# A hybrid encoder block on one core: the end of building h in halves and quarters with scans held, the passage from o to the gate by token tile, an even order in the inversions

## The chip, the cores and the metric

One core of one Trainium2 chip runs the whole kernel. The metric is the device time of one execution in microseconds (us). Three timed executions took 1959.03, 1960.29 and 1960.35 us; their median, 1960.29 us, is the time before. A fourth execution was profiled.

The engines have short names in the views: PE is TensorE (PEld its loads of stationary operands), DVE is VectorE, ACT is ScalarE, POOL is GpSimd, SP is SyncE, which issues most of the loads.

## The reference

```python
mod = silu(c) @ ada_w + ada_b                     # shift, scale, gate for mixer and FFN
h = rms_norm(x, norm_mix_w) * (1 + scale_m) + shift_m
proj = h @ w_in                                   # split into both branches, z, o, merge gates
h_a = bidirectional(mlstm_chunkwise, ...)         # 4 heads, dk 256, dv 512
y_a = (sigmoid(a_o) * rms_norm(h_a)) @ w_branch_a
o_b = bidirectional(gated_delta_chunkwise, ...)   # 16 heads, conv of 5, chunks, triangular solve
y_b = (rms_norm(o_b) * silu(b_z)) @ w_branch_b
x = x + gate_m * ((g_a * y_a + g_b * y_b) @ w_out)
hf = rms_norm(x, norm_ffn_w) * (1 + scale_f) + shift_f
gt, up = split(hf @ w_gate_up)
x = x + gate_f * ((silu(gt) * up) @ w_down)
return rms_norm(x, norm_final_w)
```

There are T = 256 tokens (two token tiles of 128) and D = 2048 features (KB = 16 blocks of 128). All is fp32.

## The kernel before

Every weight is read once from HBM, in pieces of 1 MB ("raw" tiles, three buffers, loads issued by SP). ACT rounds a half of a piece to fp32r (`wh`), DVE subtracts to get the rest (`wl = raw - wh`), and TensorE adds three products for one of fp32: wh with the high part of the activations, wh with their low part, wl with the high part. `wh` and `wl` have three buffers each. Two generators do this. `fjob` (L164) makes 128 output features with 256 tokens in a multiplication. `tjob` (L193) has a token tile as the stationary operand and 512 output features in a multiplication; it takes four pieces, so eight halves of 12 multiplications. With `by_token`, its last two halves are multiplied token tile by token tile, so that the first tile's result is done early.

Much of the rest of the work is latency: small operations that wait for one another. `fill(n)` puts n pieces of jobs between them, so that TensorE has something to do. Where `order(...)` is put around an instruction, it keeps its place in the program among those so marked on its engine; the others a scheduler places. `behind` and `settle()` hold back work, such as an evict or a SiLU, until the next half has its `wh`. `ask`, `add` and `pump` bring in the rows of ada_w for the later modulations, one 1 MB load and one DVE sum (`add`, L123) at a time.

The stages, by time in the profile:

* To 138 us, h. Per block b, SP loads two tiles of ada rows (`ra`, 1.025 MB each) and one 1 MB `raw` tile of w_in. DVE multiplies and sums the first (L519, its factor from `pk`, a table of constants) and the second (L523), and between them multiplies x by the row factors and the scale (L548). ACT adds the shift (L551) and rounds to `hh` (L552), DVE makes `hl` (L555), and TensorE adds 16 output tiles `first` in plain fp32 (L557, 32 multiplications). Table `cst` holds the identity, masks (`Dm`) and signs.
* To 300 us, `gates()` turns the first outputs into the decay and beta of the gated delta rule (GDN), with a z job and the q, k, v of the first heads between; `gdn_phase1` makes per head the decay matrices `dec` by four scans (L591 and on) and the masked products.
* To 940 us, four groups g of four heads. `invert(g)` solves the triangular 32x32 systems on DVE: 30 steps of a multiply-and-sum into `utmp` and an add into `uu` (L701, L707). The results go to DRAM (`inv_d`) and come back in another layout (`cg`, L720), and a transpose of `cg` (L722) starts `gdn_blocks`. POOL issues these transfers: the store once for the upper and once for the lower 16 rows, each as four (one per head of a group, 16 partitions each, in runs of 128 bytes); the load as four of 32 partitions in runs of 2 KB. A job is filled in between: in `gdn_invert`, a yield comes when a size that counts each step's elements plus 125 passes 580, and starts again at 0. In the groups' second half, `stream()` takes the next heads' jobs into the loops of `gdn_phase2` (n from 1 to 9, p 0 and 1).
* To 1200 us, the mLSTM branch and both branch projections.
* To 1260 us, `o_job` (the output projection), the residual and its RMS norm, and the transposes `pxn` of the normed x (L1341) into `hfh`, `hfl`, which the gate job `gt0` needs. `normed` (L1276 on DVE, L1278 on ACT) scales a token tile's columns; `block` and `pair` transpose two blocks of 128 features, both token tiles together, and scale them.
* To 1950 us, gate and up, then down; then the final norm.

## Time and profile before

| what | value |
|---|---|
| median of three executions | 1960.29 us |
| the profiled execution's own time | 1962.84 us |
| its span in the trace | 1961.0 us |
| TensorE busy | 1926.3 us, 98% |
| DVE busy | 1405.7 us, 72% |
| ACT busy | 1028.7 us, 52% |
| moved from and to HBM | 467.07 MB read, 16.82 MB written |
| mean granted clock of TensorE | 0.994 |

A row of a timeline has the start, the duration, engine, line of the code, operation, what it writes and reads, and, in brackets, how long the engine was idle before it and whose end released it. A row of a windows view has a stretch, its length, each engine's busy time with its number of instructions, the granted clock of TensorE (1.00 is full), the mean share of the DMA engines that were busy, and GB/s. A multiplication of 128x512 is shown with 0.38 us, because they overlap in a pipeline; the distance of two starts is what one costs.

### The profile page before, as it was taken

To read this page: it belongs to the slowest core of one execution; us is meant where nothing else is said; L and a number is where in the kernel's file an instruction comes from. 1 tells how busy PE (TensorE), PEld (TensorE's weight loads), DVE (VectorE), ACT (ScalarE), POOL (GpSimd) and SP (SyncE) were. 2 spreads that over 40 slices of the span, in tenths; PEclk is the share of its full clock that TensorE was granted. 3 is DMA by queue.
4 is the path that set the end of the run, shared out by engine and by line. 5 is a ranking of instruction groups with operands and counts; after the bars stand their busy time and mean duration, and the time that the engine had idled before them with its cause. 6 is when DMAs were issued, how large, how long until landed. Compare 5 with 4: busy or idle time off the path is not lost.

```text
span 1961.0 us, 27095 instructions
## 1 busy us (share of the span) xinstructions
PE 1926.3 (98%) x10418; PEld 1703.2 (87%) x10418; DVE 1405.7 (72%) x2067; ACT 1028.7 (52%) x1553; POOL 116.9 (6%) x211
## 2 busy tenths in 40 slices
PE   8999999999999999999999999999999999999997
PEld 6888889998999899889787888888888888888886
DVE  6779886898788788866677988665665665555554
ACT  3137656775776588555544444644444444444444
POOL 0001210101011101110100000200000000000000
PEclk9999999999999999999999999999999999999999
DMA  9986677666666667687777998566666665555553
GB/s 400 420 355 223 187 249 252 209 229 217 228 211 212 226 217 232 221 285 254 250 294 266 352 348 325 179 242 247 247 248 239 245 246 193 197 211 209 199 206 138
DMA packets 78962, 485.64 MB, mean 248 GB/s; under 512 B 10585, under 2 KB 15969, under 8 KB 24433
## 3 DMA queue, kind: packets, MB, share of 16 engines
q1 hardware_dynamic: 63216, 450.69, 63.0%
q0 software_dynamic: 8160, 17.88, 4.3%
q10 hardware_dynamic: 7458, 15.36, 2.0%
q8 instruction: 81, 1.33, 0.3%
q14 instruction: 47, 0.39, 0.1%
HBM read 467.07 MB, written 16.82 MB: 247 GB/s over the span
## 4 chain that ended last, share of the span: by engine, by line
PE 83%; DVE 7%; DMA 6%; ACT 2%; issue 2%; POOL 0%; SPq 0%; ACTq 0%; DVEq 0%; POOLq 0%
PE acc_gt L230 4%; PE acc_gt L231 4%; PE acc_gt L232 4%; PE acc_up L232 4%; PE acc_up L231 4%; PE acc_up L230 4%; PE acc_d L232 4%; PE acc_d L231 4%; PE acc_d L230 4%; DMA ra<-ada 3%; PE acc_b L183 3%; PE acc_b L185 3%; PE acc_b L184 3%; PE acc_o L232 3%; PE acc_o L230 3%; PE acc_o L231 2%
## 5 line engine op out<-in xcount | busy, mean ns | idle before, releaser
L211 DVE TENSOR_TENSOR wl_d<-raw_d,wh_d 128x1024 fp32r<-128x1024 f32 x88 | 107.7, 1225 | 105.9 <-ACT wh_d L209 105.9
L211 DVE TENSOR_TENSOR wl_up<-raw_up,wh_up 128x1024 fp32r<-128x1024 f32 x88 | 107.7, 1225 | 100.2 <-ACT wh_up L209 100.1
L211 DVE TENSOR_TENSOR wl_gt<-raw_gt,wh_gt 128x1024 fp32r<-128x1024 f32 x88 | 108.2, 1229 | 80.2 <-ACT wh_gt L209 80.2
L183 PE MATMUL acc_b<-hh,wh_b 128*128 128x256 f32 x576 | 163.2, 283 | 0.0
L185 PE MATMUL acc_b<-hh,wl_b 128*128 128x256 f32 x576 | 160.0, 278 | 0.0
L184 PE MATMUL acc_b<-hl,wh_b 128*128 128x256 f32 x576 | 159.5, 277 | 0.0
L209 ACT ACTIVATE wh_d<-raw_d 128x1024 fp32r<-128x1024 f32 x88 | 92.9, 1056 | 126.4 <-PE acc_d L231 117.6
L209 ACT ACTIVATE wh_gt<-raw_gt 128x1024 fp32r<-128x1024 f32 x88 | 92.9, 1055 | 118.6 <-PE acc_gt L231 71.1
L209 ACT ACTIVATE wh_up<-raw_up 128x1024 fp32r<-128x1024 f32 x88 | 92.8, 1055 | 108.1 <-PE acc_up L231 77.1
L123 DVE SCALAR_TENSOR_TENSOR ada<-ada,crow 128x2048 f32<-128x2048 f32 x64 | 146.1, 2283 | 0.0
L230 PE MATMUL acc_gt<-wh_gt,hfh 128*128 128x512 f32 x352 | 135.9, 386 | 0.0
L231 PE MATMUL acc_gt<-wh_gt,hfl 128*128 128x512 f32 x352 | 135.1, 384 | 0.0
L232 PE MATMUL acc_gt<-wl_gt,hfh 128*128 128x512 f32 x352 | 134.2, 381 | 0.0
L230 PE MATMUL acc_up<-wh_up,hfh 128*128 128x512 f32 x352 | 133.4, 379 | 0.0
L231 PE MATMUL acc_up<-wh_up,hfl 128*128 128x512 f32 x352 | 133.4, 379 | 0.0
L232 PE MATMUL acc_up<-wl_up,hfh 128*128 128x512 f32 x352 | 133.4, 379 | 0.0
L230 PE MATMUL acc_d<-wh_d,ffh 128*128 128x512 f32 x344 | 130.5, 379 | 0.0
L231 PE MATMUL acc_d<-wh_d,ffl 128*128 128x512 f32 x344 | 130.5, 379 | 0.0
L232 PE MATMUL acc_d<-wl_d,ffh 128*128 128x512 f32 x344 | 130.4, 379 | 0.0
L557 PE MATMUL first<-x,raw 128*128 128x256 f32 x512 | 114.5, 382 | 7.5 <-ACT x L551 7.5
L557 PEld LDWEIGHTS first<-x,raw 128*128 128x128 f32 x512 | 96.0, 190 | 26.0 <-ACT x L551 13.5
L183 PEld LDWEIGHTS acc_b<-hh,wh_b 128*128 128x128 f32 x576 | 111.9, 194 | 0.1
(383 smaller groups left out, 5258.0 us busy)
## 6 DMA issues: line engine op xcount, KB each, us to landing
ada<-ada SPq DMA_DIRECT2D x64, 1024.0 KB, 6.2
raw_gt<-wgu SPq DMA_DIRECT2D x44, 1024.0 KB, 5.0
raw_up<-wgu SPq DMA_DIRECT2D x44, 1024.0 KB, 4.9
raw_d<-wd SPq DMA_DIRECT2D x44, 1024.0 KB, 4.9
raw_b<-winb SPq DMA_DIRECT2D x36, 1024.0 KB, 5.3
ra<-ada SPq DMA_DIRECT2D x32, 1025.0 KB, 15.6
raw<-win SPq DMA_DIRECT2D x16, 1024.0 KB, 14.5
raw_z<-wint SPq DMA_DIRECT2D x16, 1024.0 KB, 5.1
```

The source lines that it names most:

```text
L123: order(V.scalar_tensor_tensor(raw, raw, 1.0, row_c[:, :D], ALU.mult, ALU.mult, accum_out=mod[:, c : c + 1]))
L183: PE.matmul(o, wh[:, k], woven(hh[:, kk]), start=kk == 0, stop=False)
L184: PE.matmul(o, wh[:, k], woven(hl[:, kk]), start=False, stop=False)
L185: PE.matmul(o, wl[:, k], woven(hh[:, kk]), start=False, stop=kk == KB - 1)
L209: order(S.activation(wh, raws[u][:, k0 : k0 + 2], AF.Copy), early)
L211: order(V.tensor_tensor(wl, raws[u][:, k0 : k0 + 2], wh.bitcast(F32), ALU.subtract), early)
L230: order(PE.matmul(ps[t], xh[:, kk, c], woven(wh[:, k]), start=kk == 0, stop=False), early and steps > 1)
L231: PE.matmul(ps[t], xl[:, kk, c], woven(wh[:, k]), start=False, stop=False)
L232: PE.matmul(ps[t], xh[:, kk, c], woven(wl[:, k]), start=False, stop=kk == last)
L557: PE.matmul(first[o], raw[:, o], x[:, b], start=b == 0 and o % 2 == 0, stop=b == KB - 1 and o % 2 == 1)
```

## The change

It has these parts.

* **Start.** ACT loads the identity, the 16 columns of `pk` that the h loop needs (`pkn`), and the last 13 columns of `cst`. All of `pk` is loaded by SP behind the last `raw` tile of h, the rest of `cst` behind z's first pieces.
* **h loop.** The multiply of x by the row factors is made a block ahead (`spread`), and the scale is applied by ACT together with the shift. An Exp on one column stands ahead of the loop.
* **Last block of h.** The `ra` tiles are loaded and summed in halves (1024 and 1026 columns, with an add of 128x1), and `raw` in quarters. Four of the 16 outputs stay fp32; the other twelve are split (`wh_first`, `wl_first`, three of 128x512 each) and take three fp32r multiplications each.
* **gates, phase 1.** In `gates`, the order of Abs, Exp, the first convolution, `gden` and its reciprocal is fixed; the z job makes two halves at its start instead of three. The four scans of `dec` of heads 0 and 1 come a step later.
* **Inversions.** `uu` holds the heads interleaved, so `inv_d` is stored by one DMA for each of the two halves of rows (runs of 2 KB) and `cg` is read in runs of 128 bytes. For g > 0 the yields come when the sum of elements plus 200 a step passes 765, with what is over carried on, and DVE's splits are kept in program order (`beside`). `fill(7)` after `next(blocks)` is `fill(5)` for g > 0.
* **Ahead.** In group 0, p = 1, one piece of the stream is taken ahead of the loop, and one less at n = 8.
* **o to the gate.** The o job's last three halves go by token tile (`late=3`). The gate job's first two halves of weights are split while o_3 still runs, in a pool of their own (`xq`). The norm of the first token tile, its scaling and its four transposes (`turned`) are made within the residual of the second; `hfh` and `hfl` of blocks 0 to 3 are made per token tile (`high1`, `low1`), and the gate multiplies these blocks by token tile, in the order wh with hfh, wl with hfh, wh with hfl.

The rows of an engine's program show three of these places. On DVE at the end of h and the start of z, before (`first` holds the outputs of the h loop, `cv` a convolution, `wl_z_0_0` the first split of the z job, `gden` a denominator of the gates):

```order
L523 SCALAR_TENSOR_TENSOR ra_1_671,m_15_676<-ra_1_671,crow 128x2050
L555 TENSOR_TENSOR hl<-x,hh 128x256 x2
L334 SCALAR_TENSOR_TENSOR cv_0_746<-pad_140,pk,cv_0_746 128x256 x3
L334 SCALAR_TENSOR_TENSOR cv_1_798<-pad_142,pk,cv_1_798 128x256
L334 SCALAR_TENSOR_TENSOR cv_0_746<-pad_140,pk,cv_0_746 128x256
L334 SCALAR_TENSOR_TENSOR cv_1_798<-pad_142,pk,cv_1_798 128x256
L211 TENSOR_TENSOR wl_z_0_0_703<-raw_z_0_700,wh_z_0_0_702 128x1024
L211 TENSOR_TENSOR wl_z_0_2_707<-raw_z_0_700,wh_z_0_2_706 128x1024
L334 SCALAR_TENSOR_TENSOR cv_1_798<-pad_142,pk,cv_1_798 128x256 x2
L211 TENSOR_TENSOR wl_z_1_0_713<-raw_z_1_710,wh_z_1_0_712 128x1024
L398 TENSOR_SCALAR zz<-first_237,pk,cst 128x256
L413 TENSOR_SCALAR gden<-u 128x256
```

And now, from the last half sum on (`wl_first` are the splits of the last block's twelve outputs):

```order
L548 SCALAR_TENSOR_TENSOR ra_1_676,m_15_686<-ra_1_676,crow 128x1026
L550 TENSOR_TENSOR m_15_686<-m_15_686 128x1
L593 TENSOR_TENSOR hl<-x,hh 128x256 x2
L604 TENSOR_TENSOR wl_first_703<-raw_15_677,wh_first_701 128x512
L604 TENSOR_TENSOR wl_first_704<-raw_15_677,wh_first_702 128x512 x2
L415 TENSOR_SCALAR zz<-first_241,pk,cst 128x256
L351 SCALAR_TENSOR_TENSOR cv_0_759<-pad_142,pk,cv_0_759 128x256 x2
L351 SCALAR_TENSOR_TENSOR cv_1_848<-pad_144,pk,cv_1_848 128x256
...
L215 TENSOR_TENSOR wl_z_0_0_768<-raw_z_0_765,wh_z_0_0_767 128x1024
L215 TENSOR_TENSOR wl_z_0_2_772<-raw_z_0_765,wh_z_0_2_771 128x1024
L426 TENSOR_SCALAR gden<-u 128x256
```

Three splits and `zz` now stand ahead of z's first split, and the denominator comes ahead of its third instead of behind it.

On DVE in the inversion of g = 1, before, around its longest steps (`uu` and `utmp` are the inversion's, `wl_mb` and `wl_o` splits of jobs):

```order
L211 TENSOR_TENSOR wl_mb_3_2_4054<-raw_mb_3_4027,wh_mb_3_2_4053 128x1024
L701 TENSOR_TENSOR utmp_3852<-uu_2865 64x228
L707 TENSOR_TENSOR uu_2865<-uu_2865,utmp_3852 64x19x12
L701 TENSOR_TENSOR utmp_3852<-uu_2865 64x234
L707 TENSOR_TENSOR uu_2865<-uu_2865,utmp_3852 64x18x13
L701 TENSOR_TENSOR utmp_3852<-uu_2865 64x238
L707 TENSOR_TENSOR uu_2865<-uu_2865,utmp_3852 64x17x14
L701 TENSOR_TENSOR utmp_3852<-uu_2865 64x240
L707 TENSOR_TENSOR uu_2865<-uu_2865,utmp_3852 64x16x15
L211 TENSOR_TENSOR wl_o_0_0_4082<-raw_o_0_4079,wh_o_0_0_4081 128x1024
L701 TENSOR_TENSOR utmp_3852<-uu_2865 64x240
L211 TENSOR_TENSOR wl_o_0_2_4102<-raw_o_0_4079,wh_o_0_2_4101 128x1024
```

And now, the same steps:

```order
L761 TENSOR_TENSOR utmp_3899<-uu_2909 64x228
L767 TENSOR_TENSOR uu_2909<-uu_2909,utmp_3899 64x19x12
L215 TENSOR_TENSOR wl_mb_3_0_4075<-raw_mb_3_4072,wh_mb_3_0_4074 128x1024
L761 TENSOR_TENSOR utmp_3899<-uu_2909 64x234
L767 TENSOR_TENSOR uu_2909<-uu_2909,utmp_3899 64x18x13
L215 TENSOR_TENSOR wl_mb_3_2_4093<-raw_mb_3_4072,wh_mb_3_2_4092 128x1024
L761 TENSOR_TENSOR utmp_3899<-uu_2909 64x238
L767 TENSOR_TENSOR uu_2909<-uu_2909,utmp_3899 64x17x14
L761 TENSOR_TENSOR utmp_3899<-uu_2909 64x240
L767 TENSOR_TENSOR uu_2909<-uu_2909,utmp_3899 64x16x15
L215 TENSOR_TENSOR wl_o_0_0_4122<-raw_o_0_4119,wh_o_0_0_4121 128x1024
```

Where eight instructions of the inversion stood between two splits, there are two or four.

On TensorE at the passage from o to the gate, before (`acc_o` is the o job, `pxn` a transpose of the normed x, `acc_gt` the gate job with one bank per token tile):

```order
L255 MATMUL acc_o_2_11593<-wl_o_3_2_11549,mgh 128x256
L1341 MATMUL pxn_11637<-cst,xn_11610 128x128 x2
L1341 MATMUL pxn_11643<-cst,xn_11610 128x128 x2
L1341 MATMUL pxn_11651<-cst,xn_11610 128x128 x2
L1341 MATMUL pxn_11655<-cst,xn_11610 128x128 x2
L230 MATMUL acc_gt_0_11672<-wh_gt_0_0_11554,hfh 128x512
L231 MATMUL acc_gt_0_11672<-wh_gt_0_0_11554,hfl 128x512
L232 MATMUL acc_gt_0_11672<-wl_gt_0_0_11555,hfh 128x512
L230 MATMUL acc_gt_1_11673<-wh_gt_0_0_11554,hfh 128x512
```

And now:

```order
L272 MATMUL acc_o_2_11635<-wl_o_3_2_11578,mgh 128x256
L1357 MATMUL pxn_11654<-cst,xn_11627 128x128 x4
L234 MATMUL acc_gt_0_11689<-wh_gt_0_0_11524,hfh 128x512
L234 MATMUL acc_gt_0_11689<-wl_gt_0_0_11525,hfh 128x512
L234 MATMUL acc_gt_0_11689<-wh_gt_0_0_11524,hfl 128x512
...
L234 MATMUL acc_gt_0_11689<-wh_gt_0_2_11563,hfl 128x512
L1357 MATMUL pxn_11703<-cst,xn_11627 128x128 x4
L234 MATMUL acc_gt_1_11690<-wh_gt_0_0_11524,hfh 128x512
```

Eight transposes of both token tiles stood ahead of the first gate multiplication; now four of the first tile do, and twelve gate multiplications of that tile stand ahead of the second tile's four.

The diff, cut to its core:

```diff
-    S.dma_start(cst, cst_d)
-    S.dma_start(pk, pk_d)
+    S.dma_start(cst[:, CS_ID : CS_ID + P], cst_d[:, CS_ID : CS_ID + P])
+    pkn = cp.tile([P, KB], F32, name="pkn")
+    S.dma_start(pkn, pk_d[:, PK_NMIX : PK_NFFN])
+    S.dma_start(cst[:, CS_SGN:], cst_d[:, CS_SGN:])
...
+        if lead:
+            for t in range(2):
+                for k in range(4):
+                    hi, lo = (woven(a[:, k % 2]) for a in made[k // 2])
+                    c = slice(t * P, (t + 1) * P)
+                    for a, w in ((xh, hi), (xh, lo), (xl, hi)):
+                        order(PE.matmul(ps[t], a[:, k, c], w, start=not k and w is hi and a is xh, stop=False))
...
-        size = 0
+        size, each, chunk = 0, *((200, 765) if g else (125, 580))
...
-            size += i * w + 125
-            if size > 580:
-                size = 0
+            size += i * w + each
+            if size > chunk:
+                size = size - chunk if g else 0
                 yield
...
-            G.dma_start(cg[32 * b : 32 * b + 32, 0], inv_d[g][:, b].rearrange("j x i -> j (x i)"))
+            G.dma_start(cg[32 * b : 32 * b + 32, 0], inv_d[g][16 * b : 16 * b + 16].rearrange("x j i -> j x i"))
...
+        def spans(b):
+            return (slice(0, 1024), slice(1024, D + 2)) if b == KB - 1 else (slice(0, D + 2),)
...
-            order(V.scalar_tensor_tensor(x[:, b], x[:, b], m2[:, 0:1], rows, ALU.mult, ALU.mult))
...
-            order(S.activation(x[:, b], x[:, b], AF.Identity, bias=m2[:, 1:2]))
+            order(S.activation(x[:, b], x[:, b], AF.Identity, scale=m2[:, 0, 0:1], bias=m2[:, 1, 0:1]))
             order(S.activation(hh[:, b], x[:, b], AF.Copy))
+            if b < KB - 1:
+                spread(b + 1)
...
+        for o0 in range(4, N0, 4):
+            w = [a[o0 // 8][:, o0 % 8 : o0 % 8 + 4] for a in (wh, wl)]
+            order(S.activation(w[0], raw[:, o0 : o0 + 4], AF.Copy))
+            order(V.tensor_tensor(w[1], raw[:, o0 : o0 + 4], w[0].bitcast(F32), ALU.subtract))
...
-        zj = z_job(0, 3)
+        nc.sync.dma_start(pk, pk_d)
+        zz = w0.tile([P, T], F32, name="zz")
+        opened = gates(w0, zz, first)
+        next(opened)
+        silu = behind.pop()
+        zj = z_job(0, 2)
...
+        if h < 2:
+            decay()
...
-        fill(7 if g else 8)
+        fill(5 if g else 8)
...
+            ahead = not g and p
+            if ahead:
+                next(pieces)
...
+    def share(t):
+
+        order(S.activation(ss1[:, t, 3:4], rs1[:, t : t + 1], AF.Copy))
+        normed(1, t, whole, G)
...
+            turned(0)
+
+            def first_block():
+                high1(0, 0)
+                low1(0, 0)
                 order(V.scalar_tensor_tensor(rs1[:, 4:5], sq, 1.0 / D, rs1[:, 4:5], ALU.mult, ALU.add))
-                token_rstd(rs1, 0)
-                normed(0, 0, left, S)
-
-            residual(1, 3, ps, gm, ss1, wp, True, part, rs1[:, 7:8], part, first_tile)
+                high1(0, 1)
+                high1(0, 2)
+
+            residual(1, 3, ps, gm, ss1, wp, True, part, rs1[:, 7:8], part, first_block)
             token_root(rs1, 1, 7)
...
+    next(gt0)
+    next(gt0)
+    turned(1)
+    for b in range(4):
+        high1(1, b)
+        low1(1, b)
+    next(gt0)
```

## The prediction

> **What bounds the kernel now.** I read the page first, then the waits of TensorE, then the chain, and last the stretches in which TensorE waits. The head of the page, its engine row and its chain row:

> ```profile
> span 1961.0 us, 27095 instructions
> PE 1926.3 (98%) x10418; PEld 1703.2 (87%) x10418; DVE 1405.7 (72%) x2067; ACT 1028.7 (52%) x1553; POOL 116.9 (6%) x211
> PE 83%; DVE 7%; DMA 6%; ACT 2%; issue 2%; POOL 0%; SPq 0%; ACTq 0%; DVEq 0%; POOLq 0%
> ```

> TensorE is busy for 98% of the span. The change leaves its arithmetic nearly alone, so what can be won is the 35 us in which it idles, and the time in which its clock is cut. The waits of TensorE say where (us in all, times, longest):

> ```profile
> PE first L557 <- ACT x L551: 7.5, 15, 2.4
> PE acc_mb L232 <- DVE wl_mb L211: 2.8, 3, 1.6
> PE acc_o L232 <- DVE wl_o L211: 1.5, 2, 1.1
> PE acc_z L232 <- DVE wl_z L211: 1.5, 1, 1.5
> PE pxn L1341 <- ACT xn L1278: 1.5, 1, 1.5
> PE p L767 <- DVE pt L759: 1.2, 1, 1.2
> PE acc_ma L232 <- DVE wl_ma L211: 1.0, 1, 1.0
> PE acc_v L232 <- DVE wl_v L211: 1.0, 1, 1.0
> PE pxn L1341 <- DVE xn L1276: 1.0, 1, 1.0
> ```

> Nearly every row is a place that the change touches. The first belongs to the h loop, which the loads bound, as the second row below shows.

> **The start and the last block of h.** The first multiply of ada rows (DVE) and a stretch of the h loop (us, busy time of PE, PEld, DVE, ACT, POOL, PEclk, DMA share, GB/s):

> ```profile
> 12.32 2.35 DVE L519 SCALAR_TENSOR_TENSOR ra<-ra,pk,crow 128x2050 f32<-128x2050 f32 x1 [1.27 <-DMA pk<-pk]
> 36.00:66.00 30.00, 28.76 (x130) 24.03 (x130) 21.70 (x25) 3.69 (x8) 0.00 (x0) 1.00 1.01 419
> ```

> Once the loop runs, the DMA engines are full, at 419 GB/s. So the earlier first multiply (1.27 us of waiting for pk goes) is worth only what the loads of the loop come sooner: pk and most of cst, some 0.4 MB at 1608 and 1588 bytes a partition, leave the queue ahead of them, less the pieces that are put in. At 0.42 MB/us I estimate 0.7 us; the ends are 0 and 1.27. The multiply that moves ahead of its block (L548) is 0.49 us of DVE per block, hidden already by the loads except in the last block. There:

> ```profile
> 125.19 2.35 DVE L519 SCALAR_TENSOR_TENSOR ra<-ra,pk,crow 128x2050 f32<-128x2050 f32 x1 [2.04 <-DMA ra<-ada]
> 127.59 0.49 DVE L548 SCALAR_TENSOR_TENSOR x<-x,m,rows 128x256 f32<-128x256 f32 x1
> 127.99 2.29 DVE L523 SCALAR_TENSOR_TENSOR ra<-ra,crow 128x2050 f32<-128x2050 f32 x1
> 130.32 0.51 ACT L551 ACTIVATE x<-x,m 128x256 f32<-128x256 f32 x1 [6.52 <-DVE ra L523]
> 130.88 7.17 PE L557 MATMUL first<-x,raw 128*128 128x256 f32 x32 [0.30 <-ACT x L551]
> ```

> The first ada rows land at 125.15 and the second 1.05/0.42 = 2.5 us later, at 127.65. With halves, only the last half sum stands behind that: 2.29/2 = 1.15, an add of 128x1 and the two gaps about 0.3, ACT and its gap 0.56: TensorE starts at about 129.6 instead of 130.9. Its work falls too. Of 32 multiplications at 7.17/32 = 0.224 us, 24 go, and 36 in fp32r come, at 0.112 each (from the rows below, 30 of them in 3.35 us):

> ```profile
> 387.76 0.28 PE L185 MATMUL acc_b<-hh,wl_b 128*128 128x256 f32 x1
> 391.11 0.28 PE L185 MATMUL acc_b<-hh,wl_b 128*128 128x256 f32 x1
> ```

> That is 5.38 - 4.03 = 1.35 us less. Together the block ends 2.6 us sooner, and with the start 3.3. The loop's raw quarters and the twelve splits of wh_first and wl_first hide behind the first four outputs if the last quarter lands by 130, which the same loads allow.

> **z and v, behind h.** What DVE does next, before:

> ```profile
> 133.14 2.71 DVE L334 SCALAR_TENSOR_TENSOR cv<-pad,pk,cv 128x256 f32<-128x256 f32 x6 [1.41 <-ACT cv L332]
> 135.77 2.35 DVE L211 TENSOR_TENSOR wl_z<-raw_z,wh_z 128x1024 fp32r<-128x1024 f32 x2
> ```

> The first split wl_z stands behind six convolution steps of 0.45 in both kernels, and after the change also behind zz and three wl_first. TensorE comes 3.3 us sooner, the split does not: I take a new wait of 1.1 us at the start of z (ends 0 and 2). In exchange the wait of 1.5 inside z (acc_z above), behind gden and its reciprocal, goes: they move ahead of the third split, where two splits are in hand. For acc_v, 1.0 goes (scans held for a step) and the split wl_v now stands behind eight masks of ks instead: 0, with ends -1.0 and +1.1. Sum of this stage: -0.7 - 2.6 + 1.1 - 1.5 = **-3.7** (from -0.5 to -6.4).

> **Phase g=0, p=1 (ahead).** TensorE has some two dozen multiplications of acc_b put ahead of the p that waits for pt, but DVE gets two splits (1.2 each) and an ada sum ahead of pt, so pt comes later by about as much as the new work lasts: **0**. Ends: +2 if the new work must itself wait for its split; -4.3 if the wait of 1.2 goes and with it the halved clock behind it, next.

> ```profile
> 375.30:378.70 3.40, 2.23 (x20) 2.04 (x18) 3.40 (x12) 2.67 (x9) 0.66 (x2) 1.00 0.54 201
> 378.70:385.50 6.80, 6.80 (x33) 6.80 (x33) 5.03 (x8) 3.26 (x10) 2.90 (x6) 0.50 0.67 193
> ```

> **Inversions g=1 to 3.** The rows of acc_mb, acc_o and acc_ma, 5.3 us, are waits for a split that stands behind steps of the inversion on DVE:

> ```profile
> 459.48 1.21 DVE L211 TENSOR_TENSOR wl_mb<-raw_mb,wh_mb 128x1024 fp32r<-128x1024 f32 x1
> 463.61 0.40 DVE L707 TENSOR_TENSOR uu<-uu,utmp 64x240 f32<-64x240 f32 x1
> 463.94 1.21 DVE L211 TENSOR_TENSOR wl_o<-raw_o,wh_o 128x1024 fp32r<-128x1024 f32 x1
> 465.20 0.48 PE L232 MATMUL acc_o<-wl_o,hh 128*128 128x512 f32 x1 [1.10 <-DVE wl_o L211]
> 861.03 0.48 PE L232 MATMUL acc_mb<-wl_mb,hh 128*128 128x512 f32 x1 [0.78 <-DVE wl_mb L211]
> 861.57 0.38 PE L231 MATMUL acc_mb<-wh_mb,hl 128*128 128x512 f32 x1
> 862.86 0.38 PE L231 MATMUL acc_mb<-wh_mb,hl 128*128 128x512 f32 x1
> ```

> A split and eight steps of 0.40, the last of them shown, put 4.46 us between the starts of two splits, while a half of a job lasts 12 x 0.215 = 2.58 us on TensorE (six multiplications in 1.29). The debt of 1.88 cost 1.10, so slack was 0.8. In the new order no more than four steps lie between splits in the long middle: by the same rows (4.46 less a split of 1.14 to the next start, over eight, is 0.42) 4 x 0.42 + 1.14 = 2.82, a debt of 0.24 a half, over four halves 1.0, of which some 0.3 shows: 0.9 in three inversions. The wait at 861.03 (0.78) stands behind cg and stays. 5.3 - 0.8 - 0.9 = 3.6, and 0.4 for the slower first multiplication after each of six waits (0.48 for 0.38 above): **-4.0** (from -5.7 to +1). The +1 is for cg, whose chain is:

> ```profile
> 483.17 1.32 POOL inv_d L693 x3
> 484.83 4.13 DMA inv_d<-uu
> 489.33 1.50 POOL cg L720 x3
> 490.82 5.59 DMA cg<-inv_d
> 496.80 0.71 DVE cg L722
> ```

> Three store issues fewer (1.32) help; the runs of 128 bytes move from the store to the read, which carries all 256 KB at once. The store of half as much in such runs took 4.13 for its last piece, the read in 2 KB runs 5.59: I let it cancel. [...] The profile has no such read of cg. [...]

> **From o to the gate.** The stretches there:

> ```profile
> 1242.20:1245.70 3.50, 1.57 (x13) 1.19 (x11) 2.33 (x8) 2.79 (x10) 0.00 (x0) 0.99 0.00 0
> 1245.70:1252.50 6.80, 6.22 (x18) 4.85 (x19) 5.31 (x10) 5.18 (x10) 5.87 (x4) 0.50 0.10 18
> 1244.40 0.51 ACT L1278 ACTIVATE xn<-x,rs 128x256 f32<-128x256 f32 x1 [0.30 <-DVE rs L1239]
> ```

> Two waits, 1.5 and 1.0, and then two stretches in which the clock is 0.50: 6.22 us of work that takes 3.1 at full clock. 1.5 + 1.0 + 3.1 = 5.6. After the change the first token tile's norm is done while the second's multiplications run, so its four transposes follow at once, and TensorE waits only for one ACT of 128x128, about 0.65 us with its gaps (from the 0.51 row); 12 multiplications (2.6 us) then cover most of the second tile's chain, 2.9 to 3.3 by the same rows: 0.65 more. That makes idle 1.3 in two pieces instead of 2.5, and I take it that the clock stays whole: **-4.3** (ends -5.6 and -1.2). Against that: the waits of 1.5 in z and 1.6 in acc_mb were not followed by a cut clock, that of 1.2 before p was, so the rows don't give the threshold. [...]

> **Sum:** -3.7 + 0 - 4.0 - 4.3 = -12.0 us. The profiled execution took 1962.84 us (span 1961.0), so 1950.8; the median of the runs is 2.55 lower, so 1948.3.

> **Rivals.**
> 1. The waits move instead of going: wl_z waits 2.0, wl_v 1.1 more, the inversions keep half (2.0 won), the gate passage wins 3.5: -1.7 - 2.0 - 3.5 + 0.6 for ahead = -6.6, 1953.7. For it: wl_z has more ahead of it than before. Chance 0.17.
> 2. The clock is cut at 1245 whatever the gaps (or by the new ones): 3.1 less won, 1951.4. For it: 1.3 us of gaps remain. Chance 0.12.
> 3. The change does more: in ahead the wait and the cut go too (4.3 less half a wait, 3.7): 1944.6. For it: the cut needs the window in which the idle piece lies, which moves. Against it: pt is later on DVE. Chance 0.11.
> 4. Slower: the read of cg in 128-byte runs takes over twice its 5.59 us. The transpose of cg stands in DVE's order ahead of the next split, and DVE waited for cg in the profile while TensorE lost 0.78 at 861.03, so no slack is left: each us later costs a us in each of four inversions, and over about 3 us too late the forecast's 12 is gone. At 12 us for the read: 6.4 later less 2 from the store, 4.4 x 4 = 18 and perhaps a cut clock: 1966 or more. Chance 0.06.

> **Chances.** Forecast 0.54. A measurement of this kernel tells about 0.2% (3.9 us) from no change: below 1956.4 is faster. Rivals 2 and 3 and most of 1 lie below: faster 0.85, same 0.09, slower 0.06. The range takes in rivals 1 to 3 and the bounds of the terms: the larger wins (z without a new wait, ahead's cut) to 1941, the smaller (the edges of each term taken together by half) to 1957.

> **What would show it.** In the new profile: the first z multiplication near 135 to 136 instead of 137.7; no acc_mb, acc_o or acc_ma row above 0.6 but the one behind cg; PEclk 1.00 through the 7 us behind the last o multiplication; the wait for pt still there, with 0.50 behind it. I am wrong if PEclk drops in new places, if DVE's wait for cg grows past 5 us, or if wl_z leaves a wait above 2 us.

## The result and the profile after

The forecast was 1948.3 us. The changed kernel takes **1967.62 us** (median of six runs, 1965.09 to 1971.60), the kernel before beside it 1960.32 (six runs, 1959.03 to 1962.04). The ratio is 1.0037, 95% interval 1.0027 to 1.0048: 7.3 us slower, where 12 us faster was forecast.

The profiled execution of the changed kernel is the shortest of its six (own time 1965.09), while that of before was above its median. So a second trace of before was taken (the run "before_again" below: own time 1961.23, span 1959.3), and positions are compared with that one. The head of the new page and the waits of TensorE (us in all, times, longest):

```profile
span 1963.3 us, 27151 instructions
...
PE 1925.6 (98%) x10436; PEld 1702.4 (87%) x10436; DVE 1407.5 (72%) x2086; ACT 1034.3 (53%) x1562; POOL 105.9 (5%) x187
```

```profile
PE acc_z L249 <- DVE wl_z L215: 9.7, 4, 3.4
...
PE acc_gt L234 <- DVE hfl L1372: 1.8, 2, 1.5
...
PE acc_gt L234 <- ACT hfh L1365: 1.1, 2, 0.5
...
PE acc_mb L249 <- DVE wl_mb L215: 0.8, 1, 0.8
```

TensorE is as busy as before. The acc_o and acc_ma rows are gone and acc_mb is down to its one wait behind cg, as forecast. But one row has grown to the top: acc_z (1.5 before) waits four times for its split, 9.7 us in all. Four places of the program, in the second trace of before, and the same multiplications in the trace after:

```profile
429.08 0.46 PE L230 MATMUL acc_mb<-wh_mb,hh 128*128 128x512 f32 x1
898.44 0.46 PE L183 MATMUL acc_a<-hh,wh_a 128*128 128x256 f32 x1
1241.93 0.28 PE L255 MATMUL acc_o<-wl_o,mgh 128*128 128x256 f32 x1
1254.60 0.46 PE L230 MATMUL acc_gt<-wh_gt,hfh 128*128 128x512 f32 x1
```

```profile
426.37 0.46 PE L247 MATMUL acc_mb<-wh_mb,hh 128*128 128x512 f32 x1
902.72 0.46 PE L186 MATMUL acc_a<-hh,wh_a 128*128 128x256 f32 x1
1244.34 0.28 PE L272 MATMUL acc_o<-wl_o,mgh 128*128 128x256 f32 x1
1257.83 0.48 PE L247 MATMUL acc_gt<-wh_gt,hfh 128*128 128x512 f32 x1
```

Ahead of the inversions the new kernel is 2.7 us early; behind the third it is 4.3 us late, so the three inversions cost 7.0. To the end of the o job (third row) 1.9 come back; 1.7 of them are a stretch of halved clock near 1020 us, in work that the change does not touch, which the new trace happens not to have. The passage from o to the gate costs 0.8 up to the gate's 25th multiplication (last row) and 1.5 up to its 49th (1260.66 and 1264.56), instead of winning 4.3. The spans differ by 4.0.

**The inversion of g = 1**, DVE and TensorE, with POOL's load of `uu`, after (start, duration, and in brackets the idle time before):

```profile
439.36 0.51 POOL L729 DMA_DIRECT2D uu<-inst_d  x1 [1.47 <-DMA inst_d<-mi]
...
445.50 0.16 DVE L761 TENSOR_TENSOR utmp<-uu 64x30 f32<-64x30 f32 x1 [5.63 <-issue]
...
446.85 1.21 DVE L215 TENSOR_TENSOR wl_z<-raw_z,wh_z 128x1024 fp32r<-128x1024 f32 x1
...
448.12 0.70 PE L249 MATMUL acc_z<-wl_z,hh 128*128 128x512 f32 x2 [3.37 <-DVE wl_z L215]
```

and before:

```profile
444.03 1.20 DVE L211 TENSOR_TENSOR wl_z<-raw_z,wh_z 128x1024 fp32r<-128x1024 f32 x1
446.45 1.23 DVE L211 TENSOR_TENSOR wl_z<-raw_z,wh_z 128x1024 fp32r<-128x1024 f32 x1 [1.22 <-ACT wh_z L209]
449.21 0.20 DVE L701 TENSOR_TENSOR utmp<-uu 64x30 f32<-64x30 f32 x1 [1.54 <-DMA uu<-inst_d]
```

DVE idles 5.63 us for the load of `uu` in the new kernel (issued at 439.36, landed 6.1 us later, when the first step starts), and the split that TensorE needs stands behind the first steps. Before, two splits were made while the load was on its way. DVE's order shows it; before:

```text
L594 SCALAR_TENSOR_TENSOR dec8_4783<-al8_3592,cst_78 128x128
L211 TENSOR_TENSOR wl_z1_2_0_3941<-raw_z1_2_3938,wh_z1_2_0_3940 128x1024
L211 TENSOR_TENSOR wl_z1_2_2_3963<-raw_z1_2_3938,wh_z1_2_2_3962 128x1024
L696 MEMSET uu1_2865 64x32
L701 TENSOR_TENSOR utmp1_3852<-uu1_2865 64x30
```

and after:

```text
L653 SCALAR_TENSOR_TENSOR dec8_4824<-al8_3631,cst_78 128x128
L756 MEMSET uu1_2909 64x32
L761 TENSOR_TENSOR utmp1_3899<-uu1_2909 64x30
L767 TENSOR_TENSOR uu1_2909<-uu1_2909,utmp1_3899 64x30
L761 TENSOR_TENSOR utmp1_3899<-uu1_2909 64x58
L767 TENSOR_TENSOR uu1_2909<-uu1_2909,utmp1_3899 64x58
L761 TENSOR_TENSOR utmp1_3899<-uu1_2909 64x84
L767 TENSOR_TENSOR uu1_2909<-uu1_2909,utmp1_3899 64x84
L215 TENSOR_TENSOR wl_z1_2_0_3986<-raw_z1_2_3983,wh_z1_2_0_3985 128x1024
```

The splits were unpinned before, and the scheduler had moved two of them ahead of the memset, whose successor waits for a DMA. Pinned, they stay where the program has them: behind the steps of the first yield. The same place costs 2.3 and 3.3 us of waiting in g = 2 and 3. The load of `uu` is not slow by its new layout: it takes 6.1 us from issue to landing here, and 5.9 to 6.4 in seven runs with the old one (below), 5.0 and 5.2 in the two traces of before. Windows of the new trace over the waits and what follows, and over the passage (length; busy PE, PEld, DVE, ACT, POOL; granted clock, DMA share, GB/s):

```profile
443.20:446.61 3.41, 1.55 (x8) 1.01 (x6) 0.97 (x6) 1.06 (x1) 0.00 (x0) 1.00 0.37 91
446.61:450.02 3.41, 1.90 (x9) 1.69 (x10) 3.20 (x10) 0.09 (x1) 0.00 (x0) 1.00 0.00 0
...
627.50:630.90 3.40, 1.26 (x6) 1.13 (x7) 3.16 (x10) 0.00 (x0) 0.00 (x0) 1.00 0.16 22
630.90:634.30 3.40, 3.40 (x10) 2.65 (x9) 3.26 (x8) 1.06 (x1) 0.00 (x0) 0.50 0.21 36
808.40:811.80 3.40, 0.64 (x3) 0.21 (x2) 1.93 (x8) 0.65 (x1) 0.00 (x0) 1.00 0.25 93
811.80:815.20 3.40, 2.85 (x7) 2.31 (x8) 3.23 (x9) 0.00 (x0) 0.00 (x0) 0.51 0.00 0
...
1248.70:1252.20 3.50, 3.44 (x9) 2.70 (x10) 1.67 (x7) 0.60 (x2) 1.67 (x1) 0.51 0.00 0
```

Behind the second and third wait the clock is halved for 3.4 us, which by my estimate, half of that, costs up to 1.7 us each; behind the first, the longest, it is not. The last row is the passage, where I had said that the clock would stay whole.

**The passage** in the trace after:

```profile
1245.60 0.48 PE L234 MATMUL acc_gt<-wh_gt,hfh 128*128 128x512 f32 x1 [0.55 <-ACT hfh L1365]
1246.03 0.81 ACT L1365 ACTIVATE hfh<-pxn,mod,affn 128x128 fp32r<-128x128 f32 x2 [0.48 <-DVE hf L1371]
1247.50 0.44 ACT L1365 ACTIVATE hfh<-pxn,mod,affn 128x128 fp32r<-128x128 f32 x1
1247.97 0.41 DVE L1371 TENSOR_SCALAR hf<-pxn,affn,mod 128x128 f32<-128x128 f32 x1 [1.25 <-ACT hfh L1365]
1248.76 0.79 PE L234 MATMUL acc_gt<-wh_gt,hfl 128*128 128x512 f32 x1 [1.47 <-DVE hfl L1372]
```

ACT's second `hfh` waits for DVE's first `hf` (0.48), and DVE's second `hf` waits for ACT's fourth `hfh` (1.25), which stands behind the square and the root of the other token tile. The four transposes of a token tile lie in one PSUM tile (`px` in `turned`), which both engines read, and they take turns at it in the order of the program; four_banks, below, puts that at 2.2 us. The wait that ended last is that for `hfl`, 1.47, and not the one for ACT that I had priced.

**The start** after:

```profile
133.32 2.98 DVE L351 SCALAR_TENSOR_TENSOR cv<-pad,pk,cv 128x256 f32<-128x256 f32 x7 [0.61 <-ACT cv L349]
135.76 0.38 PE L247 MATMUL acc_z<-wh_z,hh 128*128 128x512 f32 x1
136.22 2.36 DVE L215 TENSOR_TENSOR wl_z<-raw_z,wh_z 128x1024 fp32r<-128x1024 f32 x2
137.49 0.70 PE L249 MATMUL acc_z<-wl_z,hh 128*128 128x512 f32 x2 [0.70 <-DVE wl_z L215]
```

z begins at 135.76 (forecast 135 to 136), its first split is late by 0.70 behind the convolution (forecast 1.1), and the wait of 1.5 inside z is gone.

### The profile page after: what moved, and what is told of

Read it like the earlier page. It is cut to its first block, busy times and chain, and to the rows that moved or that the text cites. A ratio compares the mean times of both kernels' runs of the same rounds, so it can differ in the third digit from the quotient of the medians.

```text
span 1963.3 us, 27151 instructions
## 1 busy us (share of the span) xinstructions
PE 1925.6 (98%) x10436; PEld 1702.4 (87%) x10436; DVE 1407.5 (72%) x2086; ACT 1034.3 (53%) x1562; POOL 105.9 (5%) x187
## 4 chain that ended last, share of the span: by engine, by line
PE 84%; DVE 6%; DMA 5%; ACT 3%; issue 1%; POOL 0%; SPq 0%; ACTq 0%; DVEq 0%; POOLq 0%
PE acc_up L248 4%; PE acc_up L247 4%; PE acc_up L249 4%; PE acc_gt L248 4%; PE acc_d L249 4%; PE acc_d L248 4%; PE acc_gt L249 4%; PE acc_d L247 4%; PE acc_gt L247 4%; DMA ra<-ada 3%; PE acc_o L247 3%; PE acc_o L248 3%; PE acc_o L249 3%; PE acc_b L186 2%; PE acc_b L188 2%; PE acc_b L187 2%
## 5 line engine op out<-in xcount | busy, mean ns | idle before, releaser
L247 PE MATMUL acc_gt<-wh_gt,hfh 128*128 128x512 f32 x344 | 131.6, 383 | 0.0
L595 PE MATMUL first<-x,raw 128*128 128x256 f32 x488 | 110.0, 385 | 5.8 <-ACT x L587 5.7
L188 PEld LDWEIGHTS acc_b<-hh,wl_b 128*128 128x128 f32 x576 | 111.1, 193 | 1.9 <-DVE wl_b L183 1.9
```

The source lines that it names most:

```text
L188: PE.matmul(o, wl[:, k], woven(hh[:, kk]), start=False, stop=kk == KB - 1)
L247: order(PE.matmul(ps[t], xh[:, kk, c], woven(wh[:, k]), start=kk == 0, stop=False), early and steps > 1)
L595: PE.matmul(first[o], raw[:, o], x[:, b], start=b == 0 and o % 2 == 0, stop=b == KB - 1 and o % 2 == 1)
```

## The experiments

Each time is a median with the ratio to the kernel before, run in turns on the same chip, and its 95% interval; 0.001 is 2 us. "Four tiles" means that each of the four transposes has a PSUM tile of its own; "old layout" that `uu`, `inv_d` and `cg` are laid out, stored and read as before the change; "pieces" are what `fill` counts: each is a half with its split and 12 multiplications, 2.6 us of TensorE. Waits are the idle times in brackets of the rows; the expectations have them 0.1 to 0.2 longer. The diffs show the deciding lines.

### First four: which part loses

**pin_off**: the splits unpinned again.

```diff
-        beside[0] = g > 0
+        beside[0] = False
```

> The changed kernel, but the splits in the inversions are not kept in program order. Theory A (the waits of 3.5, 2.4 and 3.5 us at the start of the three inversions, and two cut clocks of 1.6 and 1.2 us behind them, come from the pinned split that stands behind the memset and steps of uu, which wait for the load of uu): these 12.2 us go, but the order bunches four steps (eight instructions) between splits again, so some 4 us of the old waits return: about 8 us less than the changed kernel, 1959 to 1960. Rival B (uu is loaded later, through its strided layout, and less is filled ahead): the three waits stay, 1966 to 1968.

Measured: 1966.30, 1.0030 (1.0015 to 1.0045). The waits at the start are gone, but others come; the longest lies behind cg in g = 3. Its row in the timeline, and the window that follows (columns as above):

```profile
860.97 0.79 PE L249 MATMUL acc_mb<-wl_mb,hh 128*128 128x512 f32 x1 [3.24 <-DVE wl_mb L215]
```

```profile
860.20:870.50 10.30, 9.53 (x26) 7.88 (x27) 5.38 (x6) 6.58 (x12) 0.00 (x0) 0.50 0.72 266
```

Behind those 3.24 us the clock is halved for 10.2 us, and acc_o and acc_ma wait again. I put the wait down to the two pieces that the change takes away behind the load of `cg` (`fill(5)` for `fill(7)`), but that is not shown: pin_late, next, has the same five pieces and no such wait. In pin_off the read of cg in g = 3 takes 7.0 us from issue to landing, in the change 5.2 and in pin_late 5.6; why is open. So the pin is the cause of the waits at the start, but taking it away altogether does not bring the time back. The expectation failed: rival B's time came out, but not its mechanism, for the three waits are gone.

**pin_late**: the pin begins with the third piece of an inversion.

```diff
-        for _ in gen:
+        for n, _ in enumerate(gen):
             fill(1)
+            beside[0] = g > 0 and n > 0
```

> The changed kernel, but the splits are kept in program order only from the third filled piece of an inversion on, so the first two may go ahead of uu's memset. Theory A: the 12.2 us go and the even order stays: 1955 to 1956, no wait for wl_z above 1 us. Theory B: 1966 to 1968. A third, C (the even order itself gains nothing): as pin_off, 1959 to 1960.

Measured: 1961.24, 1.0004 (0.9994 to 1.0014). Waits of 2.1, 1.0 and 2.4 are left at the start, one of them with a halved clock. With the first splits free of the load of `uu`, 6.4 of the 7.3 us are back by the medians. The trace says where: from the same multiplications as above, 429 us to 898 us in the kernel before, pin_late loses 0.5 and the change 7.0. The start of the inversions is where the change loses. The expected 1955 to 1956 did not come, since this only undoes the loss.

**old_gate**: all of the change but the passage, which is as before (`late=2`, gate without `lead`, `normed` and `block` as they were).

> The changed kernel with the passage from o to the gate as it was before. Theory A (the new passage loses what it gains, because ACT and DVE read one PSUM tile in turns, each waiting for the other): 1 to 2 us less than the changed kernel, 1965 to 1967. Rival D (the passage gains about the 4.3 us forecast and the loss lies elsewhere): 1971 to 1973.

Measured: 1966.82, 1.0033 (1.0021 to 1.0045). The change's 1.0037 lies within this interval: the new passage as built wins nothing.

**four_banks**: the change with four tiles.

```diff
-        px = gps(f"pxn_{t}")
+        px = [gps(f"pxn_{t}_{b}")[:, :P] for b in range(4)]
```

> The changed kernel, but the four transposes of a token tile go to four PSUM tiles instead of one. Theory A: ACT no longer waits for DVE between blocks, the wait for hfl of 1.6 us and most of the 0.7 us ones go, and with them the cut clock behind them: 3 to 5 us less than the changed kernel, 1963 to 1965. Rival E (the chain of the second tile's norm sets the end, not the turns): less than 1 us, 1967.

Measured: 1965.21, 1.0024 (1.0014 to 1.0034). Its waits for hfl at the gate (1.8 in the change), two rows of the passage, and the window around it:

```profile
PE acc_gt L234 <- DVE hfl L1372: 0.5, 2, 0.3
```

```profile
1250.16 0.28 PE L272 MATMUL acc_o<-wl_o,mgh 128*128 128x256 f32 x1
...
1260.25 0.48 PE L247 MATMUL acc_gt<-wh_gt,hfh 128*128 128x512 f32 x1
```

```profile
1248.00:1262.00 14.00, 12.28 (x67) 8.95 (x67) 11.35 (x30) 9.61 (x25) 7.84 (x5) 1.00 0.06 26
```

From the last o multiplication to the 25th of the gate it is 10.1 us, where the change takes 1257.83 - 1244.34 = 13.5 and before 1254.60 - 1241.93 = 12.7. The clock is whole. Only the tiles differ, so the shared one held the passage back. Other runs bear it out: the passage is 10.1 us in all nine traces with four tiles; with one tile it is 13.5 in the two traces whose clock is halved there (the change and fill6) and 12.3 in the three whose clock is whole (pin_off, pin_late, old_layout). So the turns cost 2.2 us, and the halved clock 1.2 more. In time the four tiles give 2.4 us here, a little under the expected 3 to 5. The halved clock elsewhere differs too; behind the first inversion this trace has 6.8 us of it:

```profile
446.70:453.50 6.80, 5.30 (x13) 4.21 (x14) 6.49 (x16) 1.06 (x1) 0.00 (x0) 0.50 0.21 48
```

### Next four: pieces ahead of the inversions, and the first stage alone

**fill6**: six pieces ahead of an inversion for every g, so that the load of `uu` has landed.

```diff
-        fill(4 if g else 6)
+        fill(6)
```

> The changed kernel with six pieces instead of four filled ahead of the inversions g=1 to 3; the pin stays. Theory A (the split pinned behind the steps of uu, with too little ahead of it): two more halves, 5.2 us of TensorE, cover the load of uu, so all three waits for wl_z go (9.4 us) and the clock cuts behind them: 1956 to 1958, against 1961 with the pin from the third piece on, where 6.0 us of these waits were left. Rival F (the waits only move to where the pieces run out, behind cg): 1961 to 1964, with a wait for a split behind the transpose of cg above 2 us.

Measured: 1965.63, 1.0031 (1.0016 to 1.0045). No wait at the start of an inversion is left, and yet nothing is won; neither expectation gave this time. Two pieces more are used in each inversion, and the jobs run out sooner, at the end of the groups, where TensorE then has nothing to put between:

```profile
952.00 0.59 PE L898 MATMUL px<-cst,on 128*128 128x128 f32 x2 [3.64 <-DVE on L925]
```

The clock is halved for 10.2 us behind it, and acc_a waits 2.0 behind cg in g = 1.

**fill6_four**: the same with four tiles. 

> The changed kernel with six pieces ahead of the inversions and four PSUM tiles for the transposes. Theory A: both losses gone, 1952 to 1955, faster than the kernel before by more than 0.2%. Rival G (cut clocks come in other places, as they did with the four tiles alone, where 17 us of 0.50 stood behind the waits of the inversions): 1957 to 1960.

Measured: 1963.64, 1.0016 (1.0006 to 1.0027), 2.0 us below fill6: that is what the tiles are worth in time. Both expectations were too low.

**fill6_four_old_layout**: the same, old layout.

```diff
-            G.dma_start(cg[...], inv_d[g][16 * b : 16 * b + 16].rearrange("x j i -> j x i"))
+            G.dma_start(cg[...], inv_d[g][:, b].rearrange("j x i -> j (x i)"))
...
```

> As fill6_four, but uu, inv_d and cg in the layout of before (four stores, load of cg in 2 KB runs). If the layout as a whole is neutral (the prediction): within 1.5 us of fill6_four. If the finer runs of the load of cg cost, as the fourth rival had it: 3 us or more faster. If fewer issues help: 1 to 3 us slower. Time from issue to landing: uu back from 6.1 to 5.2 us, cg from 4.4 to 5.2.

Measured: 1960.30, 1.0001 (0.9992 to 1.0011), another 3.3 us less. In this order the new layout loses.

**h_only**: the change's start, h loop, gates and held scans; inversions, layout, ahead and passage as before.

> Only the start, the h loop, gates and the held scans of the change; inversions, ahead and the passage as before. The prediction's term for them is -3.7 us, the changed kernel's trace gives 3.4 to 4.7 by 376 us: 1956 to 1957. Rival H (this stage's gain is given back later, in the waits of the inversions): 1959 to 1961.

Measured: 1959.28, 0.9993 (0.9984 to 1.0003); its span, 1956.2, is 3.1 below the second trace of before, and a multiplication of the v job stands 3.4 sooner, at 172.05 instead of 175.46:

```profile
172.05 0.38 PE L249 MATMUL acc_v<-wl_v,hh 128*128 128x512 f32 x1
```

```profile
175.46 0.48 PE L232 MATMUL acc_v<-wl_v,hh 128*128 128x512 f32 x1 [1.38 <-DVE wl_v L211]
```

The second row is from before_again. The trace shows what was forecast. The timing does not tell it from nothing: its interval reaches from 0.6 us slower to 3.1 faster, and 1956 to 1957 was expected. The profiled execution is the shortest of its ten, so the trace flatters the term; what takes the rest in the others is not settled.

### Next four: an order that is even, and what the layout costs in it

**even12_four_old_layout**: a yield at 880 instead of 765 (12 instead of 14 in an inversion), six pieces ahead, four tiles, old layout. **even12_four**: the same with the new layout.

```diff
-        size, each, chunk = 0, *((200, 765) if g else (125, 580))
+        size, each, chunk = 0, *((200, 880) if g else (125, 580))
```

> As fill6_four_old_layout (six pieces ahead of the inversions, the pin, four PSUM tiles, layout of before), but 12 yields in an inversion instead of 14 (a size of 880 instead of 765), so that the same number of pieces is used as in the changed kernel. Theory F as fill6 showed it (pieces run out at the end of group 3: waits of 0.8, 0.9 and 3.8 us at 940 to 952 us and 10 us of cut clock behind them): these 10 us go, 1950 to 1953. Rival (the cut clock there is chance): 1957 to 1960.

> As even12_four_old_layout with the layout of the changed kernel (one store, cg in runs of 128 bytes). If the finer runs cost 3.3 us as between fill6_four_old_layout and fill6_four: 1953 to 1956. If they cost only where pieces run out: within 1 us of even12_four_old_layout.

Measured: 1960.42, 1.0005 (0.9997 to 1.0013), and 1968.04, 1.0050 (1.0034 to 1.0066): 7.6 us between the layouts. Neither came to its expected 1950 to 1953 and 1953 to 1956. With the old layout the wait of 3.6 us at 952 is gone, as expected, and yet the time is that of fill6_four_old_layout: waits of 0.5 to 1.8 behind cg have come instead. DVE in g = 1 and the reads of `cg` (count, KB each, us from issue to landing), two fences with the old layout, then two with the new, and TensorE's longest wait there:

```profile
496.15 0.71 DVE L785 STREAM_TRANSPOSE cg<-cg 128x512 f32<-128x512 f32 x1 [4.69 <-DMA cg<-inv_d]
```

```profile
cg<-inv_d POOLq DMA_DIRECT2D x4, 64.0 KB, 5.8
```

```profile
496.20 0.71 DVE L782 STREAM_TRANSPOSE cg<-cg 128x512 f32<-128x512 f32 x1 [7.16 <-DMA cg<-inv_d]
```

```profile
cg<-inv_d POOLq DMA_DIRECT2D x4, 64.0 KB, 7.2
```

```profile
PE acc_a L188 <- DVE wl_a L183: 4.6, 1, 4.6
```

The read in runs of 128 bytes takes 1.4 us longer here, DVE stands still for 7.16 us, and in each of the three inversions TensorE waits 3.6 to 4.6 behind it (old layout: 0.5 to 1.8).

**old_inv_four**: the change with inversions and layout as before (125, 580, no pin, `fill(7)`), and four tiles.

> The changed kernel with the four PSUM tiles and the inversions as before (yields by 580, no pin, seven pieces behind, layout of before). Against even12_four_old_layout it gives what the even order is worth where nothing runs out. The prediction's -4.0: 1954 to 1957. Rival (the even order wins nothing): as even12_four_old_layout.

Measured: **1957.79, 0.9990 (0.9981 to 0.9998)**, the lowest time of all, faster than both kernels, by 2 us over the one before, and 2.6 below even12_four_old_layout: the even order wins nothing here. Against h_only its trace stands at the same point behind the piece taken ahead (0.04 us apart). At the end of o it is 0.6 behind, after a stretch of halved clock near 1018 us that falls to it and not to h_only. Its passage is 10.1 us instead of 12.4 up to the 25th gate multiplication, of which 0.7 is given back up to the 49th; there the lead is 1.0.

**before_again** is the kernel before, once more, for its trace. 

> The kernel before once more, for a second trace. If the trace of before that the prediction used is typical: z starts at 137.7 us, the clock is cut for 6.8 us at 378 and at 1246. If it was an unlucky one (its own time was 2.5 us above the median): less of 0.50, and a time near 1960.

Measured: 1961.23. The halved clock near 380 us lasts 3.4 us here and 6.8 in the first trace, and that behind o likewise, in the same program.

### Last four: is it the layout, and does any even order win?

Open by then were whether the layout alone explains the change's loss, and whether an even order with enough pieces behind it wins what I forecast.

**old_layout**: the change, old layout, nothing else. 

> The changed kernel with uu, inv_d and cg in the layout of before (pin, four pieces ahead, five behind stay). Theory A (the waits of the changed kernel at the inversions stand ahead, behind the pin, and leave the chain of cg time): the three waits for wl_z stay and the total is within 2 us of the changed kernel, 1966 to 1968. Rival J (the layout is the loss, as 3.3 and 7.6 us between the pairs of kernels with six pieces ahead suggest): 1960 to 1964.

Measured: 1968.72, 1.0031 (1.0018 to 1.0045). Waits of 3.6, 3.2 and 4.0 at the start of the inversions, and the clock halved behind each, for 6.8 us behind the second (below) and third:

```profile
629.90:636.70 6.80, 5.67 (x13) 4.55 (x14) 6.51 (x14) 1.06 (x1) 0.00 (x0) 0.50 0.24 73
```

In the change itself the layout is not the cause: with the old one the loss is the same. TensorE is late enough by the pin that `cg` has time.

**even10_four_old_layout** and **even10_four**: yields at 1060 (10 of them), six pieces ahead and seven behind, four tiles; old and new layout.

```diff
...
-        fill(5 if g else 8)
+        fill(7 if g else 8)
```

> Six pieces ahead of an inversion, 10 yields (size 1060), seven pieces behind as before, the pin, four PSUM tiles, the layout of before: as many pieces as the changed kernel, and more cover on both sides. Against old_inv_four (1957.8) it gives what an even order wins when nothing else is taken away. Prediction's mechanism: -2 to -4, 1954 to 1956. Rival K (with 10 pieces DVE has 15.9 + 10 x 1.14 = 27.3 us of work beside 25.8 us of TensorE, so the waits stay, spread out): 1957 to 1959.

> As even10_four_old_layout, with the layout of the changed kernel. If the finer runs only cost where too few pieces stand behind the inversion: within 1.5 us of even10_four_old_layout, for seven pieces (18 us) cover a cg that lands 7 us after its issue. If they cost anyhow: 3 us or more above it.

Measured: 1961.97, 1.0004 (0.9995 to 1.0013), and 1961.80, 1.0007 (0.9997 to 1.0018). Both lie above what was expected of the first. No wait over 0.4 us is left behind cg in either, though the reads take 4.0 and 6.4 us in g = 1: seven pieces cover the slower read too. But with fewer yields more steps lie between splits, and small waits fill the middle, here those of one job of even10_four_old_layout; acc_ma, acc_o and acc_a have 2.1, 1.5 and 1.3:

```profile
PE acc_mb L249 <- DVE wl_mb L215: 2.7, 5, 0.8
```

**even12_mid**: five pieces ahead, 12 within, six behind, the size starting at 150 so that the first yield comes sooner; four tiles, old layout. 

> Between the two: five pieces ahead, 12 yields, six pieces behind (23 as in the changed kernel), the pin, four PSUM tiles, the layout of before. If the cover on both sides is what an even order lacks: waits of about 1 us ahead and under 1 us behind an inversion instead of 6.1 us in old_inv_four, so 1954 to 1956, 3 us less than old_inv_four. Rival (TensorE has no pieces to spare, every even order gives back what it wins): 1957 to 1961.

Measured: 1958.57, 0.9993 (0.9984 to 1.0002). Waits of 1.7, 1.1 and 1.8 at the start, of 0.5 to 0.7 in the middle, and none over 0.4 behind cg; its trace has no halved clock between 22 and 1946 us. It is the best of the even orders, and no better than the old inversions; the rival's time came out.

## Why the prediction was wrong

**Start, h, z and v: right by the trace.** -3.7 was forecast, -3.4 measured (h_only at the v job); by time h_only leaves room for 3.1 at most. At 426 us the changed kernel has 2.7 left of it and old_inv_four 3.4; four_banks and pin_late, whose program is the change's up to there, have 2.9 and 2.2, so as much is the spread of executions. Inside the sum, z began 2.0 to 2.1 us sooner instead of 3.3; the new wait on wl_z took 0.7, not 1.1; the wait inside z went, and v's was 0.8 instead of 1.0 to 1.4.

**Ahead: right in size.** 0 was forecast; old_inv_four and h_only stand 0.04 apart behind it. But the wait for pt, which was to stay, is gone, and one of 1.7 for wl_b stands there, which the forecast had priced at up to +2; the clock is halved behind that as it was before.

**Inversions: the step that failed**, with -4.0 forecast and +7.0 measured by the trace. The prediction said: "In the new order no more than four steps lie between splits in the long middle". That holds, and the acc_o and acc_ma rows are gone. But it counted only what lies between splits, and not what the first pinned split stands behind: the memset and three steps of two instructions, the first of which waits for the load of `uu`, 6.1 us from issue to landing. Before, two splits lay ahead of it, since the scheduler was free to put them there. TensorE, which had taken 5.3 us in small waits, now waits 3.4, 2.3 and 3.3 at once, and two stretches of halved clock follow. pin_late shows it: with the first splits free again, 6.4 us come back.

What the runs add is that an even order wins nothing here even without that mistake. Five versions of it lie between 0.9993 and 1.0050, and old_inv_four, with the old order, at 0.9990. The pieces are a fixed stock: with two more ahead of the inversion, some are missing at 952 us (fill6); with only five behind it, cg is uncovered in most orders (even12_four, though not pin_late); with fewer within it, the distances are longer (even10). Each cure moved the wait, as my first rival had it, only further than its 6 us. That the stock is what limits every order is argued from these cases; no run had more pieces.

**Layout: "I let it cancel" was right in the changed kernel only.** There 0.8 is left behind cg, as before. Where TensorE is not late, the fourth rival's mechanism acts at a smaller size: reads of 6.4 to 7.2 us instead of 4.0 to 5.8, and 7.6 us of time in even12_four. No run shows the +1 that ends the range of the inversions for cg, nor the 2 us that the fourth rival takes off for the store. What the four pairs of runs that differ in the layout alone show, in g = 1, is reads 0.4 to 2.4 us longer with the new one, and stores of 4.7, 5.8, 4.2 and 3.6 us where the old one has 3.8, 5.3, 3.7 and 3.7.

**Passage: the second step that failed**, -4.3 forecast, +0.8 to +1.5 by trace and nothing by time (old_gate). "TensorE waits only for one ACT of 128x128" was wrong: two engines read one PSUM tile in turns (the rows of 0.48 and 1.25 idle, and 2.2 us by the runs with one tile and with four), `hfl` came 1.5 late, and the clock was halved after all, which is the second rival's outcome by another cause. With four tiles it is 10.1 us instead of 12.7, -2.6 by trace up to the 25th multiplication and -1.9 up to the 49th: the plan was sound, its sharing was not read, and its size was too large. Of the forecast, 3.1 came from 6.8 us of halved clock, which the three other traces with the old passage have for 3.4.

Along the trace, -2.7 ahead of the inversions, +7.0 in them, -1.9 up to the end of o and +1.5 in the passage make +3.9; the spans differ by 4.0. The medians differ by 7.3, because the trace of after is that of its shortest run, 2.5 below its median, and the second trace of before lies 0.9 above its own. Where an execution of middling length loses the rest I can't say; the halved clock falls differently in each run (four_banks, with nearly the same waits as the change, has 6.8 us of it behind its first inversion, where the change has none).

What stays open: whether the first splits, pinned ahead of the memset by hand, together with two more pieces of other work, would win the forecast's 4 us; the stock of pieces has none, so it wasn't tried.

## What to carry to other kernels

Before pinning an instruction in an engine's program, read in the built order what it will stand behind, down to the next wait for a DMA; a scheduler's freedom may be hiding a load (here one of 6.1 us, for which DVE idled 5.63). Count the work that fills latencies as a stock: what is put in one gap is missing in another, so price all gaps together. And where two engines are to work on blocks in parallel, look whether the blocks share a PSUM tile (2.2 us here).

## What the runs showed of the hardware

Where the pieces lie can be read from the granted clock. The halved stretches of the change, and then those of the first trace of before (between 30 and 1940 us; columns as above):

```profile
374.93:378.34 3.41, 3.25 (x15) 3.25 (x16) 3.41 (x5) 0.20 (x1) 2.26 (x5) 0.50 0.18 34
630.93:634.34 3.41, 3.41 (x10) 2.66 (x9) 3.27 (x8) 1.06 (x1) 0.00 (x0) 0.50 0.22 38
811.84:815.25 3.41, 2.90 (x7) 2.35 (x8) 3.24 (x9) 0.00 (x0) 0.00 (x0) 0.50 0.00 0
1248.74:1252.16 3.42, 3.40 (x9) 2.66 (x10) 1.63 (x6) 0.60 (x2) 1.67 (x1) 0.50 0.00 0
```

```profile
378.68:385.50 6.82, 6.82 (x33) 6.82 (x33) 5.05 (x8) 3.28 (x10) 2.92 (x6) 0.50 0.67 193
1020.38:1023.80 3.42, 3.42 (x10) 2.70 (x9) 0.66 (x2) 0.77 (x1) 0.00 (x0) 0.50 0.97 402
1245.66:1252.49 6.83, 6.21 (x18) 4.84 (x19) 5.34 (x10) 5.22 (x10) 5.86 (x4) 0.50 0.10 17
```

Their starts are 256.00, 180.91 and 436.90 us apart in the change, 641.70 and 225.28 before: 75, 53 and 128, then 188 and 66 times 3.413. Counted off from these starts, the longest wait of the change falls across two pieces, with TensorE busy for 1.55 and 1.90 of 3.41 us (first two rows of the windows in the section on the result), and neither is followed by a halved one; the wait of 2.3 falls into one piece, with 1.29 busy, which is. Of all pieces at full clock between 30 and 1940 us in these two traces, those with 0.62, 1.29, 1.61 and 1.87 us of busy TensorE (the change) and 1.52 and 2.25 (before) were followed by a halved one; those with 1.55 and 1.90 (the change) and 1.81 and 1.87 (before) were not. So where a wait lies counted beside its length; what else did, the traces do not show.

Of the pieces with more than 2.25 us busy, one was followed by a halved one, in the trace of before, in work that stands in both kernels: 24 multiplications of 128x1 (`pden`), which come twice in each trace, near 955 and 1020 us, and which the views count as busy time. This is the stretch near 1020 us that some traces have and others do not. First pin_late and the piece behind, then the change:

```profile
1017.23 2.73 PE L1025 MATMUL pden<-ones,mdec 128*128 128x1 f32 x24
1020.24:1023.65 3.41, 3.41 (x10) 2.69 (x9) 1.49 (x5) 0.00 (x0) 0.00 (x0) 0.50 0.88 324
```

```profile
1019.36 2.73 PE L1025 MATMUL pden<-ones,mdec 128*128 128x1 f32 x24
1020.06:1023.47 3.41, 3.41 (x26) 3.25 (x26) 2.50 (x8) 0.69 (x3) 0.00 (x0) 1.00 0.50 149
```

In pin_late all 24 lie in one piece, which ends at 1020.24; in the change they lie across the border at 1020.06, 7 and 17. In the first trace of before, where they start at 1016.55, 19 of them lie in the piece that ends at 1020.38, and the next is halved. Near 955 us they lie 15 and 9 there, 17 and 7 in the change, and the clock stays whole. The 24 multiplications are the same in all; what differs is their place among the pieces.

**The same read takes from 3.8 to 5.8 us in runs of 2 KB and from 3.9 to 7.2 in runs of 128 bytes** (256 KB in four transfers, in g = 1, over all kernels). In the three pairs of kernels that had six pieces ahead and differ in the layout alone, the short runs took 1.4, 1.9 and 2.4 us longer (7.2 and 5.8, 6.7 and 4.8, 6.4 and 4.0); between the change and old_layout it is 0.4 (4.4 and 4.0).
